# A hybrid state-space and dilated-attention layer: the last head pair block by block, fewer merge transfers, and where the z_b gate is multiplied in

## Chip, cores and metric

The kernel runs on one core of one Trainium2 chip. The metric is the device time of one launch in microseconds (us): the median of several runs, beside one execution that the hardware profiler recorded. PE is TensorE, PEld its weight loads, DVE VectorE, ACT ScalarE, POOL GpSimd, SP SyncE, which here issues most DMA transfers.

## What is computed

One layer on x of 2048 tokens by 1024, in float32. A normalised x is projected to u_a, z_a, q, k, v, z_b and two gates. One branch is a bidirectional state-space scan with a GLU behind it; the other is attention of 8 heads of 64 in three dilated patterns that are weighted against each other:

```python
q = rope_partial(rms_norm(q, q_norm_w[layer]), pos)
k = rope_partial(rms_norm(k, k_norm_w[layer]), pos)
for p_idx, (window, dilation) in enumerate(((128, 1), (512, 4), (2048, 16))):
    o, lse = dilated_band_attention(q[:, :, p_idx], k, v, window, dilation)
    outs.append(o); lses.append(lse)
wts = jax.nn.softmax(jnp.stack(lses, axis=0), axis=0)
attn = jnp.einsum('gblh,gblhd->blhd', wts, jnp.stack(outs, axis=0)).reshape(bsz, L, ATTN_WIDTH)
y_b = (attn * jax.nn.silu(z_b)) @ w_proj_attn[layer]
...
y_a = (glu_val * jax.nn.sigmoid(glu_gate) * jax.nn.silu(z_a)) @ w_proj_ssm[layer]
mix = jax.nn.sigmoid(g_a) * y_a + jax.nn.sigmoid(g_b) * y_b
x = x + mix @ w_out[layer]
```

## The kernel before

Matrix products are split into high and low parts and done as three matmuls (`mm3`, 314). The kernel has three stages.

**Stage a** (`phase_a`) does the projections and the scan and leaves q, k, v, the gates (GA, GB) and ZA, ZB in DRAM.

**Stage b** (`phase_b`, 1298) is attention, with other work beside it. The heads go in four pairs, hp 0 to 3. `attn_steps` (938) lists the steps: for each pair the patterns p = 1, 0, 2; a pattern has four quads (blocks of 512 queries), of two steps for p = 1 and 0 and one step for p = 2, so 20 steps a pair, 80 in all. The loop at 1310 is a pipeline of three: step i computes scores (`attn_scores`, 954), step i-1 has its probabilities transposed on PE (`attn_turn`, 1017), step i-2 is multiplied with v (`attn_values`, 1035) and copied (1058) to O[1], O[0] or, for p = 2, an `o2` tile of its own (three buffers). After each of the three comes `run`, which issues a share of the *filler*: further projections, then the GLU (`glu`, 1165), then `mix_early` (1331), the state-space part of the last projection for the first two blocks (`ssm_part`, 1367; 96 matmuls of 256 columns each).

The three patterns are weighted in **merges**. When a pair's p = 1 or p = 0 is done, `attn_stats` (1064) transposes its row statistics and writes them to ST in DRAM. When a quad of p = 2 is done, `attn_merge` (1077) starts for that pair and quad. It is a generator of three pieces, one taken at the head of each later step: (1) transpose the statistics, write ST, read back `s6` for all patterns; (2) nine small operations on DVE and ACT make the weights `e`, which two transfers write to AL (1107), six read back spread over partitions as three `ab` tiles (1110; four buffers), and one loads `zb` (1112); (3) four products and sums on POOL and one on DVE (1116 to 1121) and the store to ACTB (1122). `behind` (line 66) orders a piece's DVE and ACT work after the last marked instruction of the scores or of the mix. After the 80 steps, four rounds of 8 us of filler each advance the merges that are left (TAIL), then the rest of the filler is issued.

**Stage c** (`phase_c`, 1375) goes over eight blocks b of 256 tokens; blocks 2r and 2r+1 need quad r of all four pairs. `cut` (1342) loads ACTB into a `pair` tile (two buffers, shared with ACTA) and splits it in high and low; `proj` (1352) multiplies it by w_pa; the gates are applied and added; for b < 6 `ssm_part` of block b+2 follows; then four output tiles of 24 matmuls of 512 columns with w_out, and the residual. The 16 pieces of w_out come through three `raw` buffers that take the place of `o2`, and are split (310, 311) into tiles that lie where attention's scratch pools were. A tile framework orders each engine's and each queue's instructions by a simulated time and sets all waits, so each queue is served strictly in that order.

## Time and profile before

| | |
|---|---|
| median of 3 runs | 2058.95 us (2057.04 to 2066.33) |
| profiled execution, its own time | 2057.8 us |
| span in the profile, first to last instruction | 2056.0 us |
| PE busy | 1960.6 us (95%), granted clock 0.978 |
| PEld, DVE, ACT, POOL busy | 1762.9, 1283.1, 722.2, 838.7 us |
| DMA | 312.55 MB, mean 152 GB/s |

The time stands 1.8 us over the span, for what lies around it. Busy shares are averages over stages with different limits. The granted clock is a share of full speed: TensorE runs at 2.4 or at 1.2 GHz, and a mean between 0.5 and 1 over a stretch says how much of it was at which. A number in brackets behind an instruction of a timeline is the time that its engine sat idle before it, with the instruction or transfer that ended the wait.

### The profile page before, as it was taken

How to read it: one execution, taken by the hardware profiler on the slowest of the kernel's cores; microseconds unless marked ns; L12 is line 12 of the kernel's file. 1: busy time of each engine (PE TensorE's matmuls, PEld its weight loads, DVE VectorE, ACT ScalarE, POOL GpSimd, SP SyncE). 2: the span in 40 equal slices, each digit the busy share in tenths (PEclk: the TensorE clock that was granted, in tenths of full speed). 3: DMA queues.
4: the chain of work that ended last, by engine and by line, in shares of the span. 5: the costliest groups of instructions: out<-in, count | busy, mean ns of one | idle time of the engine just before them, and what ended most of it. 6: DMA issues, size and time to landing. Idle time of an engine off the chain costs nothing.

```text
span 2056.0 us, 37526 instructions
## 1 busy us (share of the span) xinstructions
PE 1960.6 (95%) x13612; PEld 1762.9 (86%) x13612; DVE 1283.1 (62%) x3276; ACT 722.2 (35%) x1789; POOL 838.7 (41%) x1128
## 2 busy tenths in 40 slices
PE   6899999999999999899998999999998978999999
PEld 6788899999787889899987878878887978899997
DVE  8867584878657688577765445456677656333332
ACT  4221242333222233233325545445665623101110
POOL 4410465548645755375543347457355232000000
PEclk9999999999999999999999999999999989999999
DMA  6632465346533454634465476567777447433332
GB/s 195 196 99 74 129 194 150 111 122 172 166 113 109 132 174 123 183 111 134 132 210 167 130 207 179 176 179 209 232 186 202 133 144 238 133 118 114 113 113 77
DMA packets 272059, 312.55 MB, mean 152 GB/s; under 512 B 86594, under 2 KB 182226, under 8 KB 271874
## 3 DMA queue, kind: packets, MB, share of 16 engines
q1 hardware_dynamic: 250914, 260.39, 42.3%
q0 software_dynamic: 20960, 49.76, 8.2%
q8 instruction: 108, 1.77, 0.4%
q14 instruction: 77, 0.63, 0.1%
HBM read 202.12 MB, written 105.71 MB: 150 GB/s over the span
## 4 chain that ended last, share of the span: by engine, by line
PE 62%; DVE 15%; DMA 12%; SPq 3%; POOL 3%; issue 3%; ACT 2%; DVEq 0%; POOLq 0%; ACTq 0%
PE acc L53 42%; PE po L53 11%; PE s L53 3%; PE pp L56 3%; DVE wlo L311 2%; DMA ab<-AL 2%; DMA raw<-in_w_in 1%; DMA ACTA<-fth 1%; DMA raw<-in_w_out 1%; PE y L53 1%; DMA AL<-e 1%; DVE zs L843 1%; DMA ST<-sr 1%; PE tp L56 1%; DVE zs L841 1%
## 5 line engine op out<-in xcount | busy, mean ns | idle before, releaser
L53 PE MATMUL acc<-xh,whi 128*128 128x512 f32 (+1 forms) x960 | 376.4, 393 | 18.1 <-DVE xsc L379 8.7
L53 PE MATMUL acc<-whi,xh 128*128 128x256 f32 x1280 | 368.3, 288 | 4.6 <-ACT qr L451 3.6
L53 PE MATMUL acc<-xl,whi 128*128 128x512 f32 (+1 forms) x960 | 366.5, 382 | 1.1 <-DVE xl L208 1.1
L53 PE MATMUL acc<-xh,wlo 128*128 128x512 f32 (+1 forms) x960 | 365.1, 381 | 0.0
L53 PE MATMUL acc<-whi,xl 128*128 128x256 f32 x1280 | 364.5, 285 | 0.4 <-POOL xl L263 0.4
L53 PE MATMUL acc<-wlo,xh 128*128 128x256 f32 x1280 | 364.6, 285 | 0.0
L53 PEld LDWEIGHTS acc<-whi,xh 128*128 128x128 f32 x1280 | 247.7, 194 | 7.7 <-ACT qr L451 4.2
L53 PEld LDWEIGHTS acc<-whi,xl 128*128 128x128 f32 x1280 | 247.7, 194 | 0.8 <-POOL xl L263 0.6
L53 PEld LDWEIGHTS acc<-wlo,xh 128*128 128x128 f32 x1280 | 248.0, 194 | 0.0
L53 PEld LDWEIGHTS acc<-xh,whi 128*128 128x128 f32 x960 | 184.3, 192 | 55.1 <-issue 12.0
L1014 ACT ACTIVATE p<-p,st 128x256 f32<-128x256 f32 (+2 forms) x384 | 173.2, 454 | 141.7 <-DVE st L1010 140.2
L311 DVE TENSOR_TENSOR wlo<-raw,whi 128x512 fp32r<-128x512 f32 x168 | 149.2, 906 | 107.2 <-ACT whi L310 106.4
L53 PEld LDWEIGHTS acc<-xh,wlo 128*128 128x128 f32 x960 | 183.7, 192 | 33.9 <-issue 0.4
L53 PEld LDWEIGHTS acc<-xl,whi 128*128 128x128 f32 x960 | 184.4, 192 | 28.9 <-DVE xl L208 1.5
L310 ACT ACTIVATE whi<-raw 128x512 fp32r<-128x512 f32 x176 | 102.9, 627 | 166.5 <-DMA raw<-in_w_in 141.5
L1010 DVE CUSTOM_DVE_ANT_0 p<-s,m 128x256 f32<-128x256 f32 (+2 forms) x376 | 116.1, 358 | 67.1 <-PE s L53 54.4
L53 PE MATMUL s<-kh,q 128*128 128x256 f32 (+3 forms) x400 | 105.4, 301 | 15.5 <-DVE st L1010 8.6
L53 PE MATMUL acc<-pair,wsh 128*128 128x256 f32 x512 | 100.1, 297 | 15.3 <-DVE cm L1372 10.7
L978 POOL DMA_DIRECT2D v<-V x150 | 92.6, 622 | 33.5 <-PE po L53 16.7
L53 PE MATMUL s<-kl,q 128*128 128x256 f32 (+3 forms) x400 | 103.1, 297 | 0.0
L56 PE MATMUL pp<-c_ident,p 128*128 128x128 f32 x640 | 92.8, 279 | 10.7 <-DVE t L1032 5.0
L53 PEld LDWEIGHTS acc<-pair,wsh 128*128 128x128 f32 x512 | 86.0, 205 | 17.3 <-issue 6.4
(333 smaller groups left out, 4383.3 us busy)
## 6 DMA issues: line engine op xcount, KB each, us to landing
raw<-in_w_in SPq DMA_DIRECT2D x176, 256.0 KB
q<-QT POOLq DMA_DIRECT2D x92, 256.0 KB, 4.2
ab<-AL SPq DMA_DIRECT2D x96, 128.0 KB
ug<-U SPq DMA_DIRECT2D x128, 64.0 KB
GA<-th SPq DMA_DIRECT2D x32, 256.0 KB
GB<-th SPq DMA_DIRECT2D x32, 256.0 KB
raw<-GB SPq DMA_DIRECT2D x32, 256.0 KB
xres<-in_x SPq DMA_DIRECT2D x32, 256.0 KB
```

The source lines that it names most:

```text
L53: return self.nc.tensor.matmul(*a, **k)
L56: return self.nc.tensor.transpose(*a)
L310: self.nc.scalar.activation(hi, t, AF.Copy)
L311: (eng or self.nc.vector).tensor_sub(lo, t, f(hi))
L841: V.tensor_tensor_scan(zs[:64, n, 2:258], r[:64].to_broadcast([64, 256]), z[:64, n], 0.0, op0=OP.mult, op1=OP.add)
L843: V.tensor_tensor_scan(zs[64:, n, 0:256][:, ::-1], r[64:].to_broadcast([64, 256]), z[64:, n, ::-1], 0.0, op0=OP.mult, op1=OP.add)
L978: (nc.gpsimd if late else nc.sync).dma_start(v[:(16 if p == 0 else 4) * (j1 - j0), m - m0], at(self.V, (base + 4 * j0) * C + c0, rows + [[ ...
L1010: self.marks["dve"] = nc.vector.tensor_tensor_reduce(pt, sc, mk, op0=OP.add, op1=OP.min, scale=-0.125, scalar=least if o else 3e38, accum_ ...
L1014: self.marks["act"] = nc.scalar.activation(pt, pt, AF.Exp, bias=st[:, 0, h, c:c + 1], scale=-1.0, accum_out=st[:, 1, h, c:c + 1])
```

## The change

- Pair 3 goes (p 1, quad 0), all of p 0, then for quad 0 to 3 p 1 and p 2 in turn, without the first. Its p = 1 statistics are kept in a tile for each quad and written for each quad.
- The merges' pieces 2 and 3 are taken after `attn_turn` of a step, no longer at its head. Piece 1 stays at the head.
- The weights lie in AL by pair and quad. One transfer writes them, two read them back, into one tile `ab` of three patterns (two buffers).
- The product with O[0] goes from DVE to POOL. The product with z_b and the load of `zb` leave the merge; `cut` of stage c does the product on POOL for a whole block of 128 x 1024 and splits its result. `zb` and the residual's tile come from stage c's own pool.

```diff
@@ -109,7 +109,7 @@
         self.KT = scr("KT", [8, 2, 2, 64, 2048])
         self.V = scr("V", [2048, 512])
         self.ST = scr("ST", [4, 3, 2, 2, 2048])
-        self.AL = scr("AL", [4, 3, 2, 2048])
+        self.AL = scr("AL", [4, 4, 3, 2, 512])
         self.ACTA = scr("ACTA", [8, 128, 4, 256])
         self.ACTB = scr("ACTB", [4, 4, 128, 512])
 
@@ -939,12 +939,14 @@
 
         out = []
         for hp in range(4):
-            for p in (1, 0, 2):
+            order = [(p, quad) for p in (1, 0, 2) for quad in range(4)]
+            if hp == 3:
+                order = [(1, 0)] + [(0, quad) for quad in range(4)] + [(p, quad) for quad in range(4) for p in (1, 2)][1:]
+            for p, quad in order:
                 per = 4 if p == 2 else 2
-                for quad in range(4):
-                    for sub in range(4 // per):
-                        out.append(dict(hp=hp, p=p, quad=quad, sub=sub, per=per,
-                                        idx=[4 * quad + per * sub + i for i in range(per)]))
+                for sub in range(4 // per):
+                    out.append(dict(hp=hp, p=p, quad=quad, sub=sub, per=per,
+                                    idx=[4 * quad + per * sub + i for i in range(per)]))
         prev = {}
         for x in out:
             x["group"] = prev if x["sub"] else {}
@@ -979,6 +981,8 @@
                                                                at(self.V, (base + 4 * j0) * C + c0, rows + [[1, 128]]))
             if p == 2:
                 self.st[2] = self.aw.tile([128, 2, 2, 4], F32, name="st2", bufs=3)
+            elif p == 1 and x["hp"] == 3:
+                self.st[1] = self.aw.tile([128, 2, 2, 4], F32, name="st1")
             elif quad == 0:
                 self.st[p] = self.aw.tile([128, 2, 2, 16], F32, name="st")
         q, kh, kl = g["q"], self.kh, self.kl
@@ -999,7 +1003,7 @@
         for h in range(2):
             for i, t in enumerate(x["idx"]):
                 nk, mask = tiles[t][2], self.mk[tiles[t][1]]
-                c = (t, 4 * (t % 4) + t // 4, t % 4)[p]
+                c = (t, t % 4 if x["hp"] == 3 else 4 * (t % 4) + t // 4, t % 4)[p]
                 least, o = st[:, 0, h, c:c + 1], 0
                 for _, kd, kn, m0 in tiles[t][0]:
                     pt, sc, mk = x["P"][h][:, i, o:o + kn], S[h][:, i, o:o + kn], mask[:, m0:m0 + kn]
@@ -1058,20 +1062,21 @@
         (nc.scalar.copy if quad % 2 else nc.vector.tensor_copy)(o_, i_)
         if p == 2:
             self.merges.append(self.attn_merge(hp, quad, x["st"], g["o2"]))
-        elif quad == 3:
-            self.merges.append(self.attn_stats(hp, p, x["st"]))
-
-    def attn_stats(self, hp, p, st):
+        elif quad == 3 or p == 1 and hp == 3:
+            self.merges.append(self.attn_stats(hp, p, x["st"], quad))
+
+    def attn_stats(self, hp, p, st, r):
 
         nc, R = self.nc, 2048
+        n = 4 if p == 1 and hp == 3 else 16
         pp = self.pT.tile([128, 4, 128], F32, name="pp")
-        self.tr(pp[:64, 0], st.rearrange("p a h t -> p (a h t)"), self.ident)
+        self.tr(pp[:4 * n, 0], st.rearrange("p a h t -> p (a h t)"), self.ident)
         sr = self.mg.tile([64, 128], F32, name="sr", bufs=1)
-        nc.vector.tensor_copy(sr, pp[:64, 0])
+        nc.vector.tensor_copy(sr[:4 * n], pp[:4 * n, 0])
         for a in range(4):
-            o = (hp * 3 + p) * 4 * R + a * R
-            d = ([[8, 16], [128, 16], [1, 8]], [[32, 4], [128, 16], [1, 32]])[p]
-            nc.sync.dma_start(at(self.ST, o, d), sr[16 * a:16 * a + 16])
+            o = (hp * 3 + p) * 4 * R + a * R + (512 * r if n == 4 else 0)
+            d = ([[8, 16], [128, 16], [1, 8]], [[32, 4], [128, n], [1, 32]])[p]
+            nc.sync.dma_start(at(self.ST, o, d), sr[n * a:n * a + n])
         yield
 
     def attn_merge(self, hp, r, st, o2):
@@ -1101,24 +1106,20 @@
             V.tensor_add(mn, mn, t[:, 2])
             V.reciprocal(mn, mn)
             V.tensor_mul(e, e, vw(mn, 0, [[0, 3], [1, 8]]))
-        ab = {p: mg.tile([128, 512], F32, name="ab", bufs=4) for p in (2, 1, 0)}
+        ab = mg.tile([128, 3, 512], F32, name="ab", bufs=2)
+        o = (4 * hp + r) * 3072
+        nc.sync.dma_start(at(self.AL, o, [[8, 128], [1024, 3], [1, 8]]), e)
         for h in range(2):
-            o = hp * 6 * R + h * R + 512 * r
-            nc.sync.dma_start(at(self.AL, o, [[8, 64], [2 * R, 3], [1, 8]]), e[64 * h:64 * h + 64])
-        for p, t in ab.items():
-            for h in range(2):
-                nc.sync.dma_start(t[64 * h:64 * h + 64], at(self.AL, hp * 6 * R + p * 2 * R + h * R + 512 * r, [[0, 64], [1, 512]]))
-        zb = self.op.tile([128, 512], F32, name="zb", tag="zb", bufs=2)
-        nc.sync.dma_start(zb, self.ZB[r, hp])
+            nc.sync.dma_start(ab[64 * h:64 * h + 64], at(self.AL, o + 512 * h, [[0, 64], [1024, 3], [1, 512]]))
         yield
         c = slice(512 * r, 512 * r + 512)
+        ab = [ab[:, p] for p in range(3)]
         with self.behind():
             G.tensor_mul(ab[2], ab[2], o2)
             G.tensor_mul(ab[1], ab[1], self.O[1][:, c])
             G.tensor_add(ab[2], ab[2], ab[1])
-            V.tensor_mul(ab[0], ab[0], self.O[0][:, c])
+            G.tensor_mul(ab[0], ab[0], self.O[0][:, c])
             G.tensor_add(ab[2], ab[2], ab[0])
-            G.tensor_mul(ab[2], ab[2], zb)
         nc.sync.dma_start(self.ACTB[r, hp], ab[2])
         yield
 
@@ -1307,8 +1308,9 @@
             self.k_load(0, r)
         self.run(LEAD)
         self.merges = []
+        begun = []
         for i in range(n + 2):
-            self.merges = [m for m in self.merges if next(m, self) is not self]
+            new, self.merges = [m for m in self.merges if next(m, self) is not self], []
             for d, fn in enumerate((self.attn_scores, self.attn_turn, self.attn_values)):
                 j = i - d
                 if 0 <= j < n:
@@ -1317,8 +1319,11 @@
                     if d == 0 and x["p"] == 2 and x["hp"] < 3:
                         self.k_load(x["hp"] + 1, x["quad"])
                     self.run(PACE[self.part] * (P2 if steps[min(i, n - 1)]["p"] == 2 else 1.0))
+                if d == 1:
+                    begun = [m for m in begun if next(m, self) is not self] + new
         if self.part == 2:
             self.marks = {}
+        self.merges = begun + self.merges
         for _ in range(4):
             self.run(TAIL)
             self.merges = [m for m in self.merges if next(m, self) is not self]
@@ -1339,14 +1344,18 @@
             for _ in self.ssm_part(b, self.early[b]):
                 yield 0.32 if _ is None else 0.0
 
-    def cut(self, src, scale):
+    def cut(self, src, scale, by=None):
         nc, V = self.nc, self.nc.vector
         hi, lo = self.pair()
         nc.sync.dma_start(f(lo), src)
+        x = f(lo)
+        if by is not None:
+            x = by
+            nc.gpsimd.tensor_mul(x, x, f(lo))
         for q in range(2):
             s = slice(2 * q, 2 * q + 2)
-            nc.scalar.activation(hi[:, s], f(lo[:, s]), AF.Copy, scale=scale)
-            V.scalar_tensor_tensor(lo[:, s], f(lo[:, s]), scale, f(hi[:, s]), op0=OP.mult, op1=OP.subtract)
+            nc.scalar.activation(hi[:, s], x[:, s], AF.Copy, scale=scale)
+            V.scalar_tensor_tensor(lo[:, s], x[:, s], scale, f(hi[:, s]), op0=OP.mult, op1=OP.subtract)
         return hi, lo
 
     def proj(self, b, w, y, g, gate):
@@ -1388,7 +1397,10 @@
             wcut = lambda: self.wcut(ws[0], None, 2)
             for b in range(8):
                 nb, o = b // 2, 256 * (b % 2)
-                bb = self.cut(at(self.ACTB, nb * 4 * 128 * 512 + o, [[512, 128], [128 * 512, 4], [1, 256]]), 0.5)
+                zb = cr.tile([128, 4, 256], F32, name="zb", bufs=2)
+                io = nb * 4 * 128 * 512 + o, [[512, 128], [128 * 512, 4], [1, 256]]
+                nc.sync.dma_start(zb, at(self.ZB, *io))
+                bb = self.cut(at(self.ACTB, *io), 0.5, zb)
                 mx = self.mixes.pop(b)
                 mh = self.op.tile([128, 8, 256], F32R, name="mh", tag="o0")
                 ml = self.op.tile([128, 8, 256], F32R, name="ml", tag="o1")
@@ -1411,7 +1423,7 @@
                     s = 4 * (2 * (b % 2) + t) + nb
                     for n in range(2):
                         rows = [[NS * D, 128], [1, 512]]
-                        xr = self.op.tile([128, 512], F32, name="xres", tag="zb", bufs=2)
+                        xr = cr.tile([128, 512], F32, name="xres", bufs=2)
                         nc.sync.dma_start(xr, at(self.ins["x"], s * D + 512 * n, rows))
                         ps = po.tile([128, 512], F32, name="po")
                         for k in range(8):
```

## Rows read from the trace of the kernel before

**Rows 1.** Busy time by 100 us, one row of 21; the first line names the columns.

```profile
core 0: us, PE busy (x) PEld busy (x) DVE busy (x) ACT busy (x) POOL busy (x), PEclk, DMA share, GB/s
...
1600.00:1700.00 100.00, 87.08 (x720) 82.32 (x718) 56.39 (x174) 41.34 (x128) 27.22 (x29) 0.93 0.48 140
```

**Rows 2.** Busy time of special stretches, same columns.

```profile
1210.00:1240.00 30.00, 26.40 (x184) 20.33 (x183) 18.11 (x71) 13.56 (x45) 14.75 (x23) 1.00 0.60 140
1360.00:1380.00 20.00, 16.92 (x105) 13.32 (x104) 8.88 (x43) 7.92 (x27) 8.02 (x13) 0.91 0.63 139
1520.00:1540.00 20.00, 16.02 (x134) 13.82 (x131) 14.25 (x47) 12.92 (x40) 15.39 (x24) 0.83 0.79 205
1560.00:1580.00 20.00, 11.83 (x85) 11.05 (x84) 11.56 (x23) 8.32 (x22) 8.86 (x8) 0.74 0.59 177
1664.40:1761.40 97.00, 78.37 (x484) 72.79 (x484) 54.33 (x92) 22.99 (x42) 26.13 (x20) 0.88 0.66 203
1761.40:1806.20 44.80, 44.80 (x290) 40.97 (x289) 16.37 (x24) 4.84 (x8) 0.00 (x0) 1.00 0.38 118
```

**Rows 3.** Chain of waits, attention's end to last stage: start, length, what (gaps left out).

```profile
1648.29 2.83 DMA ST<-sr
...
1651.91 2.38 DMA s<-ST
...
1654.39 0.18 DVE mn L1095
...
1656.54 0.09 DVE e L1103
...
1707.43 4.25 DMA AL<-e
...
1712.32 3.35 DMA ab<-AL
...
1715.83 1.31 POOL ab L1116
...
1717.15 0.33 SPq L302
...
1744.32 5.09 DMA raw<-in_w_out
...
1784.05 2.87 PE acc L53 x24
...
1786.93 19.30 PE po L53 x85
```

**Rows 4.** Timeline of PE, instructions that waited: start, length, what, [idle before, releaser].

```profile
1370.46 1.11 PE L56 MATMUL pp<-c_ident,p 128*128 128x128 f32 x4 [3.08 <-DVE t L1032]
...
1527.83 2.04 PE L56 MATMUL pp<-c_ident,p 128*128 128x128 f32 x8 [2.68 <-ACT t L1030]
...
1568.40 0.58 PE L53 MATMUL s<-kh,q 128*128 128x256 f32 x1 [8.00 <-DVE st L1010]
...
1689.45 0.77 PE L53 MATMUL acc<-pair,wsh 128*128 128x256 f32 x2 [4.61 <-DVE cm L1372]
```

**Rows 5.** Groups by line, 1190 to 1730 us: busy, mean ns | idle before, releasers.

```profile
L1116 POOL TENSOR_TENSOR ab<-ab,o 128x512 f32<-128x512 f32 x16 | 21.1, 1319 | 80.8 <-DMA ab<-AL 71.2 <-PE s L53 5.3 <-DMA yz<-Y 4.3
...
L1119 DVE TENSOR_TENSOR ab<-ab,o 128x512 f32<-128x512 f32 x16 | 14.8, 923 | 39.4 <-DMA ab<-AL 34.6 <-POOL ab L1118 4.8
```

**Rows 6.** Timeline of PE, SP, DVE and ACT, 1519 to 1678 us.

```profile
1667.28 0.27 PE L56 MATMUL pp<-c_ident,st 128*16 128x128 f32 x1
...
1678.34 3.68 SPq L1110 DMA_DIRECT2D ab<-AL  x6
...
1519.41 0.80 DVE L1119 TENSOR_TENSOR ab<-ab,o 128x512 f32<-128x512 f32 x1 [3.18 <-DMA ab<-AL]
...
1540.63 0.58 ACT L1058 COPY o<-po 128x512 f32<-128x512 f32 x1
...
1583.44 0.69 DVE L1119 TENSOR_TENSOR ab<-ab,o 128x512 f32<-128x512 f32 x1 [1.51 <-DMA ab<-AL]
```

## The prediction

> **What bounds the kernel now.** I read the busy time by stretch first, and look for those in which TensorE (PE) isn't busy or is at the lower clock: a gain can only come from there. The hundred from 1600 us is one, with 12.9 us idle and a granted clock of 0.93 [rows 1]. Finer stretches say what each is worth [rows 2]. Steady work of the last stage (1761 to 1806 us) has PE busy for all of its 44.8 us at clock 1.00. From 1664.4, where attention and the GLU end, to 1761.4, where the second block's projection starts, 97.0 us pass with PE busy for 78.4 at a mean clock of 0.88. The work in it can be counted from the code: three `ssm_part` and one `proj` are 4 x 96 matmuls of 256 columns, the first output block 96 of 512. By the chain of waits 24 of the first take 2.87 us and 85 of the second 19.30 [rows 3], so 384 x 0.12 + 96 x 0.227 = 68 us. **29 us** are lost there: 18.6 idle, the rest PE at 1.2 GHz after its waits.
>
> Then what PE waited for, in its timeline [rows 4]: in the tail the gated evictions (`cm`), which come late because SP's queue is full of merge transfers; inside attention DVE's or ACT's evictions. Three stretches where the four merges of a head pair meet the next pair lose 3.6, 3.1 and 4.0 us of idle; two of them also a clock of 0.91 and 0.83 [rows 2], which I count as 0.09 x 20 = 1.8 and 0.17 x 20 = 3.4 us. The DVE product with O[0] sat idle 34.6 us in total for its weights [rows 5], in front of everything else on DVE. A fifth stretch, 1560 to 1580, loses 8.2 us of idle; its wait was for a score eviction [rows 4], behind the GLU, and no merge is named.
>
> **The change part by part.**
>
> *Pair 3 by blocks.* Its steps become (p1,0), four of p0, (p2,0), then p1 and p2 by turns. In steps of the loop (60 to 79) p2's blocks move from 76, 77, 78, 79 to 70, 73, 76, 79: merges 0 to 2 start 6, 4 and 2 steps earlier, merge 3 when it did. What lay in the tail four times lies there once. New: three more `attn_stats`, each a transpose, a copy and four transfers. At 0.61 us of SP for one transfer (six take 3.68 [rows 6]) that is 12 x 0.61 = 7.3 us of SP over some 60 us, beside PE. Three merges now run beside the last steps. Four merges cost 3.1 to 7.4 us in the stretches above, so I put **+2** (0 to +6); the cover is the filler, nearly used up by then.
>
> *Fewer transfers.* A merge issued 2 AL writes, 6 `ab` loads, 1 `zb` load; now 1, 2 and 0. Six fewer issues of 0.61 us are 3.7 us of SP for each merge; bytes stay the same. `ab` was four tiles at three a merge, so 1.3 merges were in flight; now two are.
>
> *DVE's product to POOL, zb's product away.* POOL keeps five operations of 1.32 us [rows 5], DVE loses one, and with it the wait on `ab` in its queue. What waits there now is POOL's next q and v loads, as before.
>
> *Later pieces behind the transposes.* The pieces' small DVE and ACT work comes after this step's scores. It costs a merge some 2 steps' worth of order, nothing on PE while another merge is in flight.
>
> For pairs 0 and 1 these three together: lost 3.6 and 3.1 + 1.8 = 8.5 us; bounds -8.5 and +3 (a new wait in POOL's queue as large as the old one on DVE). I take **-5**, since part of the idle ended on copies that stay.
>
> For pair 2 into 3: 1520 to 1540 lost 7.4, of which I take **-4**; the 8 us at 1560 stay. New there: p0 of pair 3 now comes at step 62, not 68. Its first block writes O[0] in columns of all four blocks, so the copy must wait until all four merges of pair 2 have read O[0]. That copy falls where p1's second block had its own, at 1540.6; merge 0 read O[0] at about 1519.4, merge 3 at 1583.4 [rows 6], 21 us apart for each merge. With `ab` for two merges and 6 x 1.32 = 8 us of POOL or so beside its loads I expect 11 us apart: 1519.4 + 33 = 1552, 12 us late. The next block's copy is due 12 us later, which covers about 8. **+4** (0 to +35, the latter at the old pitch).
>
> *The tail.* Merge 3 alone, step by step [rows 3]: its transpose stays at about 1667 [rows 6]; ST write 2.8, read back 2.4, weights 2.2 (1654.4 to 1656.6), AL write 4.3, `ab` 3.4 to 5, with about 4 us of SP issue and a wait for the fifth gate product (DVE's small work is ordered behind the last one issued): its first POOL product ends at about 1691, not 1717.1. There the third `w_out` piece gets its o2 buffer, 26 us earlier. From that piece to the last on the chain 32 us passed (1717.5 to 1749.4); now that ends at 1723, when PE still has the n = 0 half. So `w_out` no longer bounds; I leave 2 us in the bounds.
>
> The AL write is the row to weigh: 4.25 us from issue to landing [rows 3]. The Trainium skill (DMA: Bandwidth & Descriptors, Anatomy of one DMA) states about 2.0 us plus the bytes for a transfer, most of it the write's receipt. By it, an estimate from that page, merge 3's two write trips would be some 3 us shorter and the time as much lower, 2037. The trace's ST write of 2.83 us comes near it, its AL write doesn't; both were taken beside other traffic, and the sum goes by them.
>
> *zb's product in the last stage.* Sixteen POOL products go, eight of twice the size come, 2 x 1.32 = 2.6 us each, plus a 512 KB load. From the second block on, the pair's tile is loaded while PE has 19 us of output matmuls [rows 3]: cost nothing; without that cover 8 x 2.6 = 21 us. The first block is exposed. PE has 2 x 96 x 0.12 = 23 us of `ssm_part`, so it wants the first `proj` at 1687.5. In POOL's program order the product stands behind merge 3's five, which end at about 1691 + 4 x 1.32 = 1696, and the new `zb` tile may lie on memory that merge 3 still holds. Then product to 1699, cut to 1701: 13 us late, and some 3 us of lower clock after it (in 1560 to 1580 the clock was 0.74 [rows 2]). Bounds 2 and 16; I take **13**, near the upper, by the order in the program. Tail: -29 + 13 = **-16** (-27 to -11).
>
> Sum: -5 - 4 + 4 + 2 - 16 = **-19 us**. The profiled execution took 2057.8 us (span 2056.0), 1.15 below the median of the runs; against the median that is 2058.95 - 19 = **2040 us**.
>
> **The rivals.**
>
> *The first block isn't held* (zb's tile free, product ahead of merge 3's): the tail loses 2 instead of 13, 2040 - 11 = 2029 us. For it: the order on a queue follows a planner's simulated readiness, and SP took the third `w_out` piece after `ab` though the program has it earlier. Against: the scratch pool and the new pool share one side of memory. Chance 0.24.
>
> *Gain handed back, no change.* Merges keep a pitch of 16 us: merge 3 reads O[0] at 1519.4 + 48 = 1567, 27 late, 8 covered, so 19 where I have 4: 2040 + 15 = 2055. Or the gate loads are late because the DMA engines are full, not SP's queue (a share of 0.66 over the tail [rows 2]), and the tail gives 4 instead of 16: 2052. Chance 0.21.
>
> *Slower: O[0] is the new wait.* At the old pitch of 21 us the first p0 copy waits until 1583, 43 late; 35 of it uncovered, the clock falls behind it as after the 8 us wait, some 5 more. 2040 + 31 + 5 = 2076 us. It decides from a pitch of about 17.5 us (27 + 4.5 late) on. For it: only one `po` bank and an in-order DVE stand behind that copy. Against: with two merges in flight and three SP issues in place of nine, the old pitch has lost its two reasons. Chance 0.12.
>
> That the change doesn't do what it says: hardly, as transfers and order are plain in the diff.
>
> **How the numbers follow.** A measurement of this kernel can tell about 0.5%, 10 us, from no change. Forecast (2028 to 2048) 0.42, first rival 0.24, no change 0.21, slower 0.12; the remaining 0.01 is spread. Faster 0.66, same 0.22, slower 0.12. The forecast's own bounds (-5 from -8.5 to +3, +4 from 0, the tail from -27) reach from about 2021 up to the no-change cases; the range takes in the first rival with its better terms and the no-change cases, and leaves the slow rival out: 2016 to 2060.
>
> **What would show it.** In the tail only one merge's POOL products after attention, the third `w_out` piece near 1690, PE's waits on `cm` mostly gone, the first `proj` held by the cut of `pair` behind POOL's product by some 10 us, and first `po` near 1724. Between pairs no DVE wait on `ab`, and PE's waits at 1370 and 1527 [rows 4] shorter. The step on O[0] is right if the first p0 copy of pair 3 waits for POOL's fourth product by some 12 us, PE by some 4. It would be wrong if PE's idle time from the end of attention to the second `proj` stayed above 15 us, if a wait of over 15 us stood before that O[0] copy, or if PE's waits moved to POOL's q and v loads.

## The result and the profile after

The changed kernel takes **2078.59 us** (median of 4 runs, 2078.18 to 2085.75) against 2062.07 of the kernel before, run beside it (4 runs, 2057.04 to 2066.33): a ratio of **1.0105**, 95% interval 1.0084 to 1.0126. It is slower by 1%; forecast were 2040 us and 2016 to 2060. The profiled execution is the longest of the four, 2085.75 us with a span of 2084.0; the other three spans are 2076.3 to 2077.1, so some 7 us of what this profile shows belong to this execution alone.

Busy time of the stretches of [rows 2] in the profile after, the columns those of before. The last two lines run from the GLU's end to the second projection, and one steady block of the last stage:

```profile
core 0: us, PE busy (x) PEld busy (x) DVE busy (x) ACT busy (x) POOL busy (x), PEclk, DMA share, GB/s
1210.00:1240.00 30.00, 26.03 (x180) 21.23 (x176) 16.18 (x60) 9.70 (x33) 16.34 (x25) 1.00 0.64 154
1360.00:1380.00 20.00, 15.54 (x96) 12.89 (x95) 9.35 (x42) 7.47 (x27) 9.11 (x16) 0.92 0.64 152
1520.00:1540.00 20.00, 16.32 (x139) 15.76 (x139) 12.62 (x40) 8.62 (x26) 9.38 (x11) 0.91 0.81 197
1560.00:1580.00 20.00, 12.81 (x100) 12.40 (x98) 11.88 (x29) 9.99 (x27) 10.92 (x13) 0.87 0.98 242
1688.60:1788.90 100.30, 72.54 (x483) 67.59 (x482) 45.57 (x72) 23.46 (x40) 18.99 (x12) 0.86 0.61 192
1788.90:1833.80 44.90, 44.90 (x290) 41.06 (x289) 16.37 (x24) 4.83 (x8) 2.42 (x1) 1.00 0.42 130
```

The steady block is the same as before, so the product of z_b inside it is hidden. The tail is not shorter: 100.3 us where 97.0 stood, with PE busy for 72.5 (78.4 before). The stretches where merges meet the next pair have as much idle time as before (4.0, 4.5, 3.7 and 7.2 us against 3.6, 3.1, 4.0 and 8.2), only their clock is higher in the last two (0.91 and 0.87 against 0.83 and 0.74). Over the wider stretches 1190 to 1260 and 1340 to 1400 this execution idles more than the one before, 6.6 and 5.9 us against 3.6 and 3.1. And the GLU now ends at 1688.8 instead of 1664.4.

What PE waited for from 1040 us to the end (us in total, times, longest):

```profile
PE acc L53 <- DMA zb<-ZB: 23.5, 1, 23.5
PE pp L56 <- DVE t L1036: 10.4, 4, 6.6
PE s L53 <- DVE st L1014: 9.9, 6, 3.8
...
PE acc L53 <- DVE cm L1381: 3.7, 2, 3.5
```

The waits on `cm` have nearly gone, as forecast [rows 4], but only beside the hold: without it, in e1 below, 9.1 us of them stand. One wait of 23.5 us has taken the place of all that the tail was to gain. Its end, in the timeline of all engines (start, length, engine, line; in brackets the idle time before and what ended it):

```profile
1705.58 0.38 SPq L1350 DMA_DIRECT2D pair<-ACTB  x1
...
1731.83 0.32 SPq L1123 DMA_DIRECT2D ACTB<-ab  x1
1733.97 0.37 SPq L1402 DMA_DIRECT2D zb<-ZB  x1
1734.09 1.67 ACT L310 ACTIVATE woh<-raw 128x512 fp32r<-128x512 f32 x3 [7.17 <-DMA ACTB<-ab]
...
1737.89 2.34 POOL L1354 TENSOR_TENSOR zb<-zb,pair 128x1024 f32<-128x1024 f32 x1 [6.09 <-DMA zb<-ZB]
1740.27 1.15 ACT L1357 ACTIVATE pair<-zb 128x512 fp32r<-128x512 f32 x2 [4.51 <-POOL zb L1354]
...
1740.95 0.80 PE L53 MATMUL acc<-pair,wah 128*128 128x256 f32 x2 [23.45 <-DMA zb<-ZB]
```

The store of the last merge (`ACTB<-ab`) is issued at 1731.83. The load of z_b for the first block follows 2.14 us later, when the store has landed, though the first block needs nothing of that merge: the load of its attention output (`pair<-ACTB`) had been issued at 1705.58. Then come the load (3.9 us to POOL's start), POOL's product (2.3), the cut, and the first projection. ACT's first cut of `w_out` waited for the same store.

The last merge itself, SP's issues:

```profile
1694.37 0.65 SPq L1090 DMA_DIRECT2D ST<-sr  x1
...
1700.30 1.31 SPq L1093 DMA_DIRECT2D s<-ST  x2
...
1714.88 0.36 SPq L1111 DMA_DIRECT2D AL<-e  x1
1717.50 1.24 SPq L1113 DMA_DIRECT2D ab<-AL  x2
```

Its ST write goes out 5.6 us behind the GLU's end, its last store 43.0 us behind it; the forecast had that at 31.6 (1696 against 1664.4). Between pair 1 and 2, the groups of DVE's instructions that waited for a merge's loads (busy us, mean ns, idle us before them), 1340 to 1400 us; first before, then after:

```profile
L1119 DVE TENSOR_TENSOR ab<-ab,o 128x512 f32<-128x512 f32 x2 | 2.0, 987 | 7.8 <-DMA ab<-AL 7.8
...
L1095 DVE TENSOR_TENSOR mn<-s 128x8 f32<-128x8 f32 x4 | 0.6, 159 | 7.9 <-DMA s<-ST 7.9
```

```profile
L1100 DVE TENSOR_TENSOR mn<-s 128x8 f32<-128x8 f32 x4 | 1.1, 263 | 15.9 <-DMA s<-ST 15.9
```

DVE's wait for `ab` [rows 5] is gone, and its wait for `s6` is as much longer: 7.8 + 7.9 us have become 15.9. DVE, no longer stopped by one merge, stops at the next merge's first operation. In this stretch the longest of these waits (7.5 us) ends on loads that SP issued 5.7 us behind that merge's own ST write (1366.75 to 1372.49). Between pair 0 and 1 the loads of `s6` stand on SP behind the loads of the merge before, which wait for their AL write:

```profile
1220.91 0.43 SPq L1111 DMA_DIRECT2D AL<-e  x1
...
1228.71 1.24 SPq L1113 DMA_DIRECT2D ab<-AL  x2
1230.05 1.24 SPq L1093 DMA_DIRECT2D s<-ST  x2
```

The AL write at 1220.91 held SP until 1228.71. At 1714.88, with less beside it, the same step took 2.62 us. The Trainium skill (DMA: Bandwidth & Descriptors, Anatomy of one DMA) gives about 2.0 us as the fixed part of a transfer that GpSimd issues; the second, issued by SyncE, is near it, the first is not. Right before the first, SP had issued merge 0's weights, two loads of 384 KB, from 1218.99 on, and one load of 256 KB; that these held it is likely, and no run tests it.

Last, the wait on O[0] between pairs 2 and 3: POOL's products on O[0] of the four merges of pair 2, then DVE's copies on either side of the wait, with PE's last matmuls for the second of them:

```profile
1532.33 1.28 POOL L1121 TENSOR_TENSOR ab<-ab,o 128x512 f32<-128x512 f32 x1
...
1541.98 1.45 POOL L1121 TENSOR_TENSOR ab<-ab,o 128x512 f32<-128x512 f32 x1
...
1572.38 1.73 POOL L1121 TENSOR_TENSOR ab<-ab,o 128x512 f32<-128x512 f32 x1
...
1582.22 1.72 POOL L1121 TENSOR_TENSOR ab<-ab,o 128x512 f32<-128x512 f32 x1
```

```profile
1538.55 0.68 DVE L1062 COPY o<-po 128x512 f32<-128x512 f32 x1
...
1558.04 0.65 PE L53 MATMUL po<-t,v 128*64 128x128 f32 x6
...
1587.71 0.68 DVE L1062 COPY o<-po 128x512 f32<-128x512 f32 x1
```

From the copy of (p1,0) to the first of p0 49 us pass. PE had that block ready at 1558.7, and the copy follows the last read of O[0], which ends at 1583.9 as it did before (1584.1 by [rows 6]). The four reads end 9.8, 30.7 and 9.8 us apart, so one gap makes the wait. Before, they ended 15.8, 37.0 and 11.2 us apart; the two reads in the middle there:

```profile
1535.26 0.70 DVE L1119 TENSOR_TENSOR ab<-ab,o 128x512 f32<-128x512 f32 x1 [0.64 <-DMA ab<-AL]
...
1572.28 0.68 DVE L1119 TENSOR_TENSOR ab<-ab,o 128x512 f32<-128x512 f32 x1
```

What lies in the gap of the changed kernel:

```profile
1532.44 0.36 SPq L1111 DMA_DIRECT2D AL<-e  x1
...
1546.81 1.55 POOL L1122 TENSOR_TENSOR ab<-ab 128x512 f32<-128x512 f32 x1
...
1554.17 0.35 SPq L1193 DMA_DIRECT2D ACTA<-fth  x1
...
1556.08 0.86 SPq L1123 DMA_DIRECT2D ACTB<-ab  x1
...
1559.77 1.24 SPq L1113 DMA_DIRECT2D ab<-AL  x2
```

SP issues the write of merge 2's weights at 1532.44 and their loads 27.3 us later. There are two `ab` tiles, so the third merge needs the first one's, which its store gives back. That merge's last sum on POOL ends at 1548.4, its store goes out at 1556.08, behind a store of the GLU (`ACTA<-fth`) before which SP issued nothing for 7 us, and merge 2's loads follow. Between pair 1 and 2 it is the same: written at 1378.57, loaded at 1406.31, behind the stores at 1401.39. This is read from the trace; no run gives the merges more tiles.

### The profile page after: what moved, and what is told of

It is laid out like the page before. It is cut to its first block, busy times and chain, and to the rows that moved or that the text cites. A ratio compares the mean times of both kernels' runs of the same rounds, so it can differ in the third digit from the quotient of the medians.

```text
span 2084.0 us, 37423 instructions
## 1 busy us (share of the span) xinstructions
PE 1962.6 (94%) x13615; PEld 1767.1 (85%) x13615; DVE 1279.9 (61%) x3263; ACT 722.7 (35%) x1789; POOL 855.0 (41%) x1136
## 4 chain that ended last, share of the span: by engine, by line
PE 62%; DVE 13%; DMA 12%; POOL 4%; issue 3%; SPq 3%; ACT 2%; DVEq 0%; ACTq 0%; POOLq 0%
PE acc L53 40%; PE po L53 12%; PE s L53 4%; PE pp L56 3%; DMA raw<-in_w_in 2%; DVE wlo L311 2%; SPq L513 1%; PE y L53 1%; DMA ACTA<-fth 1%; DMA mr<-kk 1%; DMA ST<-sr 1%; DVE zs L843 1%; DMA ACTB<-ab 1%; PE tp L56 1%; DVE zs L841 1%
## 5 line engine op out<-in xcount | busy, mean ns | idle before, releaser
L53 PEld LDWEIGHTS acc<-xh,whi 128*128 128x128 f32 x960 | 184.7, 193 | 53.6 <-issue 11.2
L1354 POOL TENSOR_TENSOR zb<-zb,pair 128x1024 f32<-128x1024 f32 x8 | 19.7, 2461 | 249.0 <-DMA pair<-ACTB 242.9
L53 PE MATMUL acc<-pair,wah 128*128 128x256 f32 x512 | 95.0, 287 | 24.0 <-DMA zb<-ZB 23.5
L53 PE MATMUL acc<-pair,wgh 128*128 128x256 f32 x512 | 107.0, 305 | 8.3 <-DVE fth L1192 8.3
L56 PE MATMUL pp<-c_ident,p 128*128 128x128 f32 x640 | 92.2, 278 | 15.8 <-DVE t L1036 10.4
```

The source lines that it names most:

```text
L53: return self.nc.tensor.matmul(*a, **k)
L56: return self.nc.tensor.transpose(*a)
L1354: nc.gpsimd.tensor_mul(x, x, f(lo))
```

## The experiments

Theory H puts the loss at three places: z_b's load held until the last merge's store, the copy into O[0], DVE's wait for `s6`. The rivals stand in each expectation (the "384 KB load" there is one of the two that a merge now has). All were run beside the kernel before. The last column is the time from the end of the GLU's last matmul to the first matmul of the first projection in the profiled execution (before: 46.1, changed kernel: 52.2), read from PE's timeline.

| run | parts on | median us | before us | ratio, 95% interval | GLU to projection |
|---|---|---|---|---|---|
| e1 | order, pieces | 2058.64 | 2057.64 | 1.0009 (0.9987 to 1.0031) | 34.5 |
| e2 | pieces, transfers, z_b | 2067.79 | 2057.64 | 1.0047 (1.0027 to 1.0067) | 61.6 |
| e3 | order, transfers, z_b | 2081.88 | 2057.64 | 1.0111 (1.0071 to 1.0150) | 50.9 |
| e4 | all, z_b's tile in the gates' | 2073.41 | 2057.64 | 1.0065 (1.0042 to 1.0089) | 36.9 |
| e5 | order, pieces, z_b | 2076.25 | 2056.90 | 1.0105 (1.0087 to 1.0123) | 52.2 |
| e6 | order | 2058.68 | 2056.90 | 1.0012 (0.9999 to 1.0024) | 34.8 |
| e7 | order, pieces, O[0] on POOL | 2057.56 | 2056.90 | 1.0009 (0.9988 to 1.0030) | 32.8 |
| e8 | order with p0 later, pieces | 2051.97 | 2056.90 | 0.9980 (0.9964 to 0.9996) | 32.6 |
| e9 | e5, z_b's tile early | 2067.16 | 2057.62 | 1.0040 (1.0020 to 1.0060) | 35.7 |
| e10 | z_b | 2072.91 | 2057.62 | 1.0071 (1.0049 to 1.0093) | 65.6 |
| e11 | order with p0 later still, pieces | 2055.82 | 2057.62 | 0.9987 (0.9970 to 1.0005) | 40.5 |
| e12 | e8, z_b, its tile early | 2056.61 | 2057.62 | 0.9994 (0.9981 to 1.0007) | 30.2 |
| e13 | statistics by block | 2059.16 | 2058.19 | 0.9999 (0.9982 to 1.0017) | 45.5 |
| e14 | pieces | 2061.24 | 2058.19 | 1.0023 (1.0005 to 1.0041) | 46.1 |
| e15 | e8, O[0] on POOL | 2066.12 | 2058.19 | 1.0032 (1.0012 to 1.0052) | 32.8 |
| e16 | e1, `ab` loads from POOL's queue | 2085.73 | 2056.52 | 1.0148 (1.0120 to 1.0176) | 33.1 |
| e17 | e8, `ab` loads from POOL's queue | 2067.55 | 2056.52 | 1.0053 (1.0037 to 1.0069) | 31.6 |

"Delay at equal matmul work" in the expectations: the matmul records are summed from the front, each counted at the usual distance of its shape in the kernel before, and the times at which two kernels reach the same sum are compared.

### Parts taken back

**e1** takes the transfers and z_b's move back:

```diff
-        ab = mg.tile([128, 3, 512], F32, name="ab", bufs=2)
+        ab = {p: mg.tile([128, 512], F32, name="ab", bufs=4) for p in (2, 1, 0)}
...
+            V.tensor_mul(ab[0], ab[0], self.O[0][:, c])
...
+            G.tensor_mul(ab[2], ab[2], zb)
```

> The order of the last pair and the later pieces stay; transfers, the weights' tiles, DVE's product on O[0] and z_b's product in the merge are as before. Theory H (three places: z_b's load of the last stage held until the last merge's store, pair 3's first write of O[0] waiting for pair 2's merges, DVE's first merge operation waiting for s6): the hold of the first projection is gone, the other two stay: 2056 to 2064 us, first projection under 8 us late, the wait before pair 3's first copy into O[0] still over 8 us. Theory T (the 384 KB copies into two tiles make every merge late and are behind all three places): 2040 to 2052 us and that wait under 4 us.

2058.64 us, no change against before. H's number held, T's did not; the copy into O[0] waited as H has it (1529 to 1578). Without the two parts the tail does what was forecast:

```profile
1673.42:1707.88 34.46, 25.32 (x194) 25.01 (x193) 15.81 (x31) 8.74 (x16) 6.35 (x5) 0.85 0.74 215
1707.88:1756.82 48.94, 45.93 (x291) 40.81 (x290) 29.11 (x43) 14.17 (x24) 7.62 (x5) 1.00 0.67 210
```

34.5 us from the GLU's end to the first projection, 11.6 under before, and no wait on z_b. What it gains there, the steps before had lost: the GLU ends at 1673.4, 9 us late.

**e2** takes the order back (hp goes to 3, so `hp == 9` never holds):

```diff
-            if hp == 3:
+            if hp == 9:
...
-        elif quad == 3 or p == 1 and hp == 3:
+        elif quad == 3:
```

> The last pair in the order of before; later pieces, fewer transfers and z_b's product in the last stage stay. H: the O[0] wait between pairs 2 and 3 is gone (11 to 14 us back), the first projection is held by the last merge as long or longer: 2064 to 2074 us. T: the merges are as late as in the changed kernel and the time stays within 3 us of it, 2075 to 2082 us.

2067.79, in H's range. Its GLU ends at 1661.6, no later than before, so the late end of the GLU belongs to the new order; the first projection is then held 28.0 us.

**e3** takes the later pieces back:

```diff
-            new, self.merges = [m for m in self.merges if next(m, self) is not self], []
+            self.merges = [m for m in self.merges if next(m, self) is not self]
...
-                    begun = [m for m in begun if next(m, self) is not self] + new
```

> The merges' second and third pieces at the head of the step as before; order, transfers and z_b's product stay. H: if the later pieces are what puts DVE's wait for s6 ahead of the score reductions, the 4 us of pair 0 to 1 and the 4 us of pair 1 to 2 come back: 2068 to 2073 us. T (the pieces' place does not matter beside the transfers): 2075 to 2082 us.

2081.88: T's range, H's clause on the pieces fell. DVE waited 17.8 us for `s6` in 1340 to 1400 without the later pieces, 15.9 with them; beside the transfers their place does not matter.

### z_b's tile

**e4** keeps all parts and moves z_b's tile of the last stage:

```diff
-                zb = cr.tile([128, 4, 256], F32, name="zb", bufs=2)
+                zb = [self.ev.tile([128, 512], F32, name="zb", tag="e1") ... for _ in range(2)]
...
+                (V if first else nc.gpsimd).tensor_mul(by[q], by[q], x[q])
```

> The changed kernel, but z_b of the last stage lies in the two 2 KB tiles that the gates of the mixing used, in halves, not in a new pool over the attention's memory, and the first block's product is made on DVE. H: the first projection of the attention output starts by 1728 us into the span (1741 in the changed kernel) and the 23.5 us wait falls to under 8: 2060 to 2067 us. Rival M (the mix's tiles lie on O[0] and O[1], which the last merge reads until 1731, and the cuts of w_out on its scratch, so that the wait only moves to the third quarter of the projection): 2070 to 2076 us.

2073.41, between the two (0.4% under the changed kernel by the ratios). The first projection starts at 1721.8 as H has it, but a wait of 9.3 us stays, since the gates' last product on those tiles ends at 1713.3 and z_b's first load goes out at 1713.6, and the stretch behind it takes 54.9 us (48.0 in the changed kernel): rival M is half right.

**e5** takes the transfers alone back:

```diff
-            G.tensor_mul(ab[0], ab[0], self.O[0][:, c])
+            V.tensor_mul(ab[0], ab[0], self.O[0][:, c])
```

with the six loads and four tiles as in e1.

> The changed kernel with the transfers, the weights' tiles and DVE's product on O[0] as before; last pair's order, later pieces and z_b's product in the last stage stay. Theory C (one 384 KB load a merge lands late, and s6's load stands behind it on SP's queue): the delay against before at equal matmul work is within 4 us of none up to pair 3's first scores (after: +5 at 1503, +10 to +14 at 1541, +15 to +18 at 1583), and what stays is the hold of the first projection, 8 to 14 us: 2062 to 2070 us. Rival D (z_b's product in the last stage is the whole loss against the run of order and pieces alone): 2074 to 2080 us. Rival L (the hold is long only because C makes the last merge late): 2056 to 2061 us.

2076.25, ratio 1.0105 like the changed kernel: rival D. The transfers are worth nothing either way within the intervals (some 0.2% on each side), and e5 against e1, 1.0105 against 1.0009, puts **z_b's move at 0.96%, 20 us**, on this order. It is the same chain as in the changed kernel:

```profile
1719.33 0.32 SPq L1124 DMA_DIRECT2D ACTB<-ab  x1
1721.85 0.37 SPq L1403 DMA_DIRECT2D zb<-ZB  x1
1721.98 1.67 ACT L310 ACTIVATE woh<-raw 128x512 fp32r<-128x512 f32 x3 [3.28 <-DMA ACTB<-ab]
...
1726.15 2.34 POOL L1355 TENSOR_TENSOR zb<-zb,pair 128x1024 f32<-128x1024 f32 x1 [6.85 <-DMA zb<-ZB]
1728.52 1.15 ACT L1358 ACTIVATE pair<-zb 128x512 fp32r<-128x512 f32 x2 [4.87 <-POOL zb L1355]
...
1729.20 0.58 PE L53 MATMUL acc<-pair,wah 128*128 128x256 f32 x1 [19.29 <-ACT pair L1358]
```

**e10** has z_b's move alone on the kernel before:

```diff
-            G.tensor_mul(ab[2], ab[2], zb)
...
+            nc.gpsimd.tensor_mul(x, x, f(lo))
...
+                zb = cr.tile([128, 4, 256], F32, name="zb", bufs=2)
```

> The kernel before with z_b's product in the last stage alone, its tile in the new pool; order, pieces and transfers as before. Theory H: the load stands behind the last merge's store (1726 in the kernel before), so the first projection starts near 1735 instead of 1711: 2070 to 2082 us. Rival N (the hold needs the new order, whose last merge comes later against the GLU's end): within 5 us of before, 2053 to 2062 us.

2072.91, ratio 1.0071: H, and 15 us for z_b's move on the order of before. The load is issued 2.31 us behind the last store here too:

```profile
1717.68 0.33 SPq L1124 DMA_DIRECT2D ACTB<-ab  x1
1719.99 0.37 SPq L1399 DMA_DIRECT2D zb<-ZB  x1
...
1723.77 2.34 POOL L1351 TENSOR_TENSOR zb<-zb,pair 128x1024 f32<-128x1024 f32 x1 [6.12 <-DMA zb<-ZB]
```

The GLU ended at 1661.2; 65.6 us pass to the first projection, at a mean clock of 0.73.

**e9** is e5 with a tile that exists before the attention's memory is given back:

```diff
-                zb = cr.tile([128, 4, 256], F32, name="zb", bufs=2)
+                zb = self.op.tile([128, 4, 256], F32, name="zb", tag="zb")
...
+            (V if first else nc.gpsimd).tensor_mul(x, x, f(lo))
```

> Order, later pieces and z_b's product in the last stage; transfers as before. z_b of the last stage has one tile in the pool that lives through the attention (the room that the merges' z_b had), so its first load waits for no memory of the attention; the first block's product is on DVE, the others on POOL. Theory H (the loss is where that tile lies): the first projection starts within 38 us of the GLU's end (34.5 with the product in the merges, 52 with the tile in the new pool), the wait of 19 us before it falls under 3, and the time is that of order and pieces alone: 2054 to 2062 us. Rival Q (the product and 512 KB more of loads in the last stage cost by themselves): 2066 to 2076 us.

2067.16, ratio 1.0040: under e5 by 0.65%, over e1 by 0.3%. The wait is as H has it, the time is in rival Q's range. The hold is gone, what stays there is `cm`:

```profile
PE acc L53 <- DVE cm L1382: 10.3, 2, 8.6
```

So the place of the tile, with the first product on DVE, carries two thirds of z_b's price. The last third is not in this stretch (35.7 us); this execution is 4 us late already at 1477 and more at 1590, where z_b's move only takes instructions away, and where that comes from is open (the residual's tile, which moves along with z_b in e5 and e9, was not tried apart).

### The order's own cost

**e6** has the order alone on the kernel before:

```diff
+            if hp == 3:
+                order = [(1, 0)] + [(0, quad) for quad in range(4)] + [(p, quad) for quad in range(4) for p in (1, 2)][1:]
...
+        elif quad == 3 or p == 1 and hp == 3:
```

> The kernel before with the last pair's order alone; pieces at the head of the step, transfers and z_b's product as before. Theory A (the order wins some 16 us behind the attention and loses some 12 beside the last pair's steps, the pieces' place does nothing): within 4 us of the run of order and later pieces, 2055 to 2062 us. Rival (the later pieces are what keeps the waits between the pairs short): 2063 to 2070 us.

2058.68: theory A. The GLU ends at 1676.3, 11.7 us late, and 34.8 us later the projection starts, 11.3 sooner than before; the two cancel. PE's largest wait from 1500 to 1700 us is for the GLU's output:

```profile
PE acc L53 <- DVE fth L1196: 19.6, 3, 8.9
PE s L53 <- DVE st L1014: 4.2, 1, 4.2
```

In the kernel before, no wait of PE in that stretch was on `fth`. Two of the three (3.7 us at 1542 and 8.9 at 1573) stand while p0's copy waits for O[0], from 1533 to 1583: PE's work is then the GLU's, and it stops where ACT and DVE have not yet brought that output out.

**e13** sends pattern 1's statistics of the last pair by block, in the old order:

```diff
-        elif quad == 3:
+        elif quad == 3 or p == 1 and hp == 3:
...
+        n = 4 if p == 1 and hp == 3 else 16
```

> The kernel before with pattern 1's statistics of the last pair sent by block (three transposes and twelve small transfers more), the order of before. If these are the last pair's own loss of 12 us under the new order: 2064 to 2070 us, the delay against before at equal matmul work 6 us or more by 1684. If the order itself is (steps that wait for O[0] while TensorE runs out of GLU work): within 4 us of before, 2053 to 2062 us.

2059.16, no change: the three transposes and twelve transfers cost nothing. The 12 us are the order's.

**e8** and **e11** move p0 later in the order:

```diff
-                order = [(1, 0)] + [(0, quad) for quad in range(4)] + [(p, quad) for quad in range(4) for p in (1, 2)][1:]
+                order = [(1, 0), (1, 1)] + [(0, quad) for quad in range(4)] + [(2, 0), (2, 1), (1, 2), (2, 2), (1, 3), (2, 3)]
```

(e11: `[(1, 0), (1, 1), (1, 2)]`, the four of p0, `[(2, 0), (2, 1), (2, 2), (1, 3), (2, 3)]`.)

> Order and later pieces, transfers and z_b as before, but in the last pair the second block of pattern 1 stands before pattern 0, whose first copy into O[0] so comes two steps later; the last pair ends on patterns 1 and 2 alike. Theory W (the wait of the first pattern-0 copy for pair 2's merges delays the steps): that copy waits under 2 us and the time falls by 3 to 8 us: 2050 to 2056 us. Rival F (TensorE has filler beside that wait): within 2.5 us of the order and pieces alone, 2056 to 2061 us.

> Order and later pieces with three blocks of pattern 1 before pattern 0 (two in the run that was 0.2% under before), then pattern 2's first three blocks, then pattern 1's and 2's last; transfers and z_b as before. Theory W (the wait for O[0] stretches the last pair): the last pair's own loss, 13 us with one block ahead and 7 with two, falls below 5 and the time is 2045 to 2051 us. Rival E (three merges at once come back as the end's wait): first projection over 40 us behind the GLU's end, 2053 to 2060 us.

e8: **2051.97**, ratio 0.9980, the only run whose interval lies under before, by little. It is in W's range, but not by W's way: the first p0 copy still came at 1591, at the last read of O[0]; PE had two more steps to run beside the wait (3.5 us on `fth` in 1500 to 1700, against 15.5 in e1). e11: 2055.82, its projection 40.5 us behind the GLU, rival E.

**e12** joins e8's order and e9's tile:

```diff
+                order = [(1, 0), (1, 1)] + [(0, quad) for quad in range(4)] + [(2, 0), (2, 1), (1, 2), (2, 2), (1, 3), (2, 3)]
...
+                zb = self.op.tile([128, 4, 256], F32, name="zb", tag="zb")
```

> Both mends: z_b's tile in the pool that lives through the attention, and two blocks of pattern 1 before pattern 0; later pieces, transfers as before. H and W: the time of the run with two blocks ahead and z_b in the merges, less up to 3 us for 16 POOL products taken out of the merges: 2047 to 2053 us. Rival Q: 2060 to 2070 us.

2056.61: neither range. Sixteen POOL products taken out of the merges bring nothing over e8.

### Pieces, POOL's product, the queue

**e14** has the later pieces alone on the kernel before:

```diff
-            self.merges = [m for m in self.merges if next(m, self) is not self]
+            new, self.merges = [m for m in self.merges if next(m, self) is not self], []
...
+                    begun = [m for m in begun if next(m, self) is not self] + new
```

> The kernel before with the merges' later pieces behind the transposes, nothing else. If they do what order and pieces together showed between the pairs (3 us ahead of before at 1473 with both, 1.5 behind with the order alone): 2052 to 2056 us. If that was scatter of the runs: within 2.5 us of before, 2055 to 2060 us.

2061.24: outside both ranges, no gain, rather 0.2% slower.

**e7** and **e15** add the O[0] product on POOL to e1 and e8:

```diff
-            V.tensor_mul(ab[0], ab[0], self.O[0][:, c])
+            G.tensor_mul(ab[0], ab[0], self.O[0][:, c])
```

> Order and later pieces, and of the fewer transfers only the product on O[0] moved from DVE to POOL; six weight loads into four tiles a merge and z_b's product in the merge as before. Theory C (the single load is what makes the merges late): within 4 us of order and pieces alone, 2053 to 2062 us, DVE's wait for ab gone (8 us in pair 1 to 2) and its wait for s6 at most 3 us longer in sum. Rival P (POOL's third product a merge makes the merges late and frees O[0] later): 2064 to 2072 us, O[0]'s last read of pair 2 over 5 us later than with order and pieces alone (1578).

> Two blocks of pattern 1 before pattern 0, later pieces, and the product on O[0] on POOL; transfers and z_b in the merges as before. If DVE's wait for the weights, which the move to POOL ends, is worth something once the first copy into O[0] comes later: 2047 to 2051 us, under the 2052 of the run with DVE's product. If POOL's longer merges (O[0]'s last read of pair 2 at 1584 against 1578 to 1590) eat it: 2052 to 2057 us.

e7: 2057.56, theory C by the time; the product's place is worth nothing. C's clause on `s6` fell: in 1340 to 1400 DVE's wait for `ab` (8.1 us in e1) is gone and its wait for `s6` is 13.7 us against 6.7, so moving the product alone moves the wait. The last read of O[0] ends 6.5 us later than in e1, as rival P has it, without P's loss. e15: 2066.12, outside both: what was neutral on e1 costs 0.5% on e8 (1.0032 against 0.9980). PE waited 8.6 us once for `fth` at 1595, as in e1. The builder orders all engines anew for each edit, and these runs show that a few us at places an edit does not touch come and go with that.

**e16** and **e17** issue the merges' weight loads from POOL's queue, on e1 and e8:

```diff
-                nc.sync.dma_start(t[64 * h:64 * h + 64], at(self.AL, ...
+                nc.gpsimd.dma_start(t[64 * h:64 * h + 64], at(self.AL, ...
```

> Order and later pieces as in the first run (2058.6), but the six weight loads of a merge are issued from POOL's queue, whose engine uses them, instead of SP's. If SP's queue (a load that waits for its AL write holds s6's loads, gates and GLU stores behind it) sets how far the merges of a pair lie apart, pair 2's last read of O[0] comes by 1568 instead of 1578, DVE's wait for s6 in pair 1 to 2 falls under 4 us (6.7), and the time to 2046 to 2054 us. If POOL's own queue (q and v loads, 0.57 us of POOL for each transfer) takes over as the wait: 2060 to 2070 us and TensorE's waits for q or v show it.

> The same move to POOL's queue on the kernel with two blocks of pattern 1 before pattern 0 (2052): 2042 to 2049 us if SP's queue sets the merges' distance, 2056 to 2066 us if POOL's queue takes its place.

2085.73 and 2067.55: the rivals, and more. Until 1400 us e16 was ahead: PE was busy for all of 1190 to 1260 and 1340 to 1400 (66.4 of 70 and 56.9 of 60 us before, 67.4 and 59.8 in e17), and in the second stretch DVE waited 2.9 us for `s6` (6.7 in e1). Between those pairs, then, having the loads on SP's queue costs PE part of what the forecast hoped to win. Then POOL's queue stands in their place: 8.0 us in front of a load, up to 1432.9, for the landing of a merge's store. In pair 2 the merges read O[0] at 1540 to 1610, later than with SP's queue (1518 to 1578), and PE waited for the copy behind it in one piece:

```profile
PE po L53 <- DVE o L1062: 17.3, 1, 17.3
PE acc L53 <- DVE fth L1196: 10.1, 1, 10.1
```

POOL itself waited 21.2 us for AL writes in front of its loads (four times, 1190 to 1700) and once 13.9 us, up to 1594.6, which the profile puts down to `zb<-ZB`; the last merge's loads stood behind that. So e16 exchanges one queue for another, and can't tell what would space the merges of pair 2 if neither held them.

## Why the prediction was wrong

The forecast was -19 us; measured were +16.5 (2078.59 against 2062.07). By its steps:

- **z_b's product in the last stage, "13 us late", bounds 2 and 16: the step that failed.** PE stood 23.5 us (19.3 in e5), and the move costs 20 us by the runs. Two terms were missing. The step had the product start when merge 3's products end. It named the tile on memory "that merge 3 still holds" and priced only POOL's order. From the last merge's store on came the store's landing (2.1 us) and z_b's own load (3.9), before the product could begin. And merge 3's end was put 31.6 us behind the GLU's end where 43.0 were measured (42.3 in e5): its small transfers and DVE operations, costed at the rows' durations, stood in SP's and DVE's order behind gates and evictions of the mix. DVE began the weights at 1709.7, 9.4 us after `s6` was asked for, and was done 5.2 us later (2.2 forecast); from the loads of `ab` to POOL's start 7.1 us passed (3.4 to 5). e5 and e10 show the price of the move, e9 that the tile's place, with the first product on DVE, carries two thirds of it. The rival "the first block isn't held" asked the right question, and was answered the other way.
- **The tail, -29 without the hold (-27 with what was left in the bounds)**: right in kind, twice too large. From the GLU's end to the second projection 96.6 us passed before, 83.4 in e1: -13.2. There the first block isn't held, and the projection starts 11.6 us nearer to the GLU's end. What stays is the wait on `cm`, 9.1 us in e1, which the forecast had as mostly gone, and a clock of 0.85.
- **Pair 3's own merges, +2 (0 to 6), and the write of O[0], +4 (0 to 35):** together 12 (e6). The last read of O[0] did not come sooner. The forecast had 11 us between merges from 1519 on; 1533.6 to 1583.9 is 16.8 apart, and from a later start (in e1 1518.0 to 1578.0, 20.0 apart). These are means, as was the 21 us of before: two gaps came as forecast (9.8), the one between merges 1 and 2 (30.7) is the wait. The step counted two tiles as two merges in flight, and not that the third merge's loads wait until the first one's store has gone out on SP. Six fewer issues on SP did not shorten that. The stop of over 15 us before that copy, which the prediction named as proof against it, is there (25 us from PE's end to the last read). The statistics by block, which the +2 took in, cost nothing (e13).
- **Pairs 0 and 1, -5**: nothing came. The wait for `ab` went from DVE, as forecast, and as much came back at `s6` (15.9 us for 15.7). The prediction had "POOL's next q and v loads" as what waits there now, and did not look at the next merge's first operation in DVE's own order. e7 and e14 find no gain in the product's place or the pieces'. That there was something to win shows in e16, where PE is busy all through both stretches.
- **Issue time on SP**: the transfers as a whole are worth nothing (e5 against the changed kernel, 1.0105 both).
- **From the second block on, cost nothing**: right, 44.9 us a block as before.
- **The sum** with the measured terms: -13 (tail) + 12 (order) + 20 (z_b) + 0 = +19, against +16.5. In the two profiles the loss lies mostly ahead: the GLU ends 24 us later, of which some 7 are this execution's and 12 the order's, and 3.5 us are lost behind it, where the tail's gain and z_b's hold meet.
- **The rivals**: slower at 2076 us by O[0] had the right size for another reason. O[0]'s wait is there, but costs 12 us that the tail gives back; the time is lost to z_b.

Of the versions run, e8 is the one to keep: order with p0 later and the later pieces, without the fewer transfers and with z_b in the merges, 0.2% under before. e11, e12 and e15 share its order and did not do better, so how much of the 0.2% is the order's is not settled.

## What to carry to other kernels

When work is moved into a new stage, ask where its buffer lies: here a tile in memory that the old stage gives back waited for the old stage's last transfer, whatever the data needed, and its load, not only its arithmetic, then stood on the path. When a wait is taken off an in-order engine, read which instruction on that same engine waits next, and whether its time has a different source; here most of the wait came back (e7), and it shrank only when the loads left the queue they shared (e16). Two tiles are two pieces of work in flight only if each comes back in time: look for the store that gives a tile back, and for what stands before it in its queue. An order of steps that brings results forward also brings writes forward into buffers that are still read: the gain at one end was paid at the other (11.3 us against 11.7).

## What was not expected of the hardware

- Two loads of 384 KB in place of six of 128 KB start the first product later: merge 0's of pair 0, issued at 1218.99, let POOL start at 1227.8 (8.8 us); in e1 the six, issued from 1218.71, let it start at 1223.0 (4.3 us), the first product needing only one third. Over the merges whose first product waited for its weights it is 6.3 to 9.7 us in the changed kernel, and 3.9 to 5.0 in e1 where the six went out together.
- A step from AL's write to the next issue on the same queue took 2.6 us with little beside it and 7.8 us right behind two loads of 384 KB and one of 256 KB.
- Small edits do not add: POOL's product on O[0] was worth nothing on one order (e7 against e1) and cost 0.5% on another (e15 against e8).
